# Split products whose moving operand is read as two halves in turns

## The chip, the cores and the metric

The kernel runs on one core of one Trainium2 chip. The metric is the device time of one execution in microseconds (us), of which the median of several runs is given. Beside it stands a profile of one execution with the start and the duration of every instruction on the core's engines: PE (TensorE, matrix products), PEld (the loading of TensorE's stationary operand, the weights, which runs beside PE), DVE (VectorE), ACT (ScalarE), POOL (GpSimd) and SP (SyncE, which issues the transfers).

## The reference

One layer of a decoder trunk, for 256 tokens of width 2048, all in float32. Cut to what matters here:

```python
mod = silu(c) @ w_ada + b_ada                       # six vectors of 2048
sh1, sc1, g1, sh2, sc2, g2 = split(mod, 6)
h = layer_norm(x) * (1 + sc1) + sh1
proj = h @ w_in                                     # 2048 x 9760
y_nsa, y_ml = nsa_attention(...), mlstm(...)        # of the columns of proj
g_nsa, g_ml = split(sigmoid(merge_g), 2)            # merge_g: 4096 columns of proj
y = (g_nsa * (y_nsa @ w_br_nsa) + g_ml * (y_ml @ w_br_ml)) @ w_o
x = layer_norm(ALPHA * x + g1 * y)
h = layer_norm(x) * (1 + sc2) + sh2
a, g = split(h @ w_up, 2)                           # 2048 x 11264
a = causal_dwconv(a)                                # width 3 along the tokens
y = (silu(a) * g) @ w_down                          # 5632 x 2048
x = layer_norm(ALPHA * x + g2 * y)
```

## The kernel before

A product of a float32 activation and a float32 weight is made of three matmuls in the type fp32r, here called a *split product*. Each operand is split in a high part (a cast to fp32r, on ACT) and a low part (the value less its high part, on DVE); the three matmuls are high by high, high by low and low by high, summed in PSUM. Weights come in tiles of 128 partitions by 1024 elements (512 KB, tile `w`), are split by `load_split` into `wh` (line L143, ACT) and `wl` (L146, DVE), and are used at once. Activations are split once and stay: `hT` (the input of all projections of `w_in`), `y_nsaT`, `y_mlT`, `mgT`, `h2T`, `uTt`, each laid out with the contracted dimension in the partitions and the 256 tokens along the free dimension, high half and low half apart.

All matmuls are issued by the helper `mm` (L109). In a matmul the stationary operand (128 columns) is loaded first, and then the moving operand streams past it, one column after the other; a column of the moving operand becomes a column of the result. There are two kinds of split products:

- `mm_b`: the weights are stationary and the 256 tokens of an activation are moving. The result has channels in the partitions and tokens in columns. It makes `ps_b` (the columns of `w_in` that attention needs transposed) and `ps_up` (the up projection).
- `mm_a`: 128 tokens are stationary and the weights are moving, 512, 392 or 256 columns of them. The result has tokens in the partitions. It makes `ps_a` (the rest of `w_in`), `ps_mg` (merge gates), `ps_br` (the two branch projections), `ps_o` (the output projection) and `ps_d` (the down projection). `proj_rows` does the last two; its last 512 columns go in two chunks of 256 (`_pack_rows` lays the weights out for it).

The order of time is: modulation, layer norm and `w_in` in three groups of its contracted dimension (to some 285 us); attention and mLSTM with `ps_mg` filled in between (to 440); `ps_br`, the rest of `ps_mg`, and `ps_o` (to 640); two layer norms (to 715); then `ps_up` for 22 blocks of 128 channels, `ps_d` over them, `ps_up` for 22 more and `ps_d` over those. Beside it `ada_chunk` multiplies the 100 MB of `w_ada` on DVE (L239, L257), a tile at a time, up to 935 us. The order of PE's work is in part written out by hand (`tc.manual_schedule`) and elsewhere follows the program; a scheduler with a cost model places the instructions of ACT and DVE.

Results leave PSUM in `dest_b` and the lines that use it (`ps_b`, L813, L815 and L817), in `residual_steps` (`ps_o`, `ps_d`), and in `up` (`ps_up`). In `up` a block of 128 channels goes through a bias and scale (L1546), the convolution along the tokens as two multiply-adds (L1549, one reads a shift of one token, the other of two), SiLU (L1551), the gate (L1552), and a split into `uTt` (L1554, L1555). The constants `OFFB`, `OFFA` and `OFFN` move the start of the tiles `wh`, `wl` and others by 16, 48 or 64 elements.

## Time and profile before

| | |
|---|---|
| median of 3 runs | 1427.51 us (1427.41 to 1427.63) |
| span of the profiled execution (first to last instruction) | 1425.4 us |
| PE busy | 1411.8 us (99%), 9234 matmuls |
| PEld busy | 1267.9 us (89%) |
| DVE busy | 1054.2 us (74%) |
| ACT busy | 704.2 us (49%) |
| moved by DMA | 374.23 MB, 263 GB/s on the mean |

The profiled execution's span ends 2.1 us under the median of the runs; the runs were not profiled, and hold what lies before the first and after the last instruction. In rows of the profile, `PE ps_up L109 x912` are 912 matmuls that write the PSUM tile `ps_up`, issued on line 109. The mean duration of a matmul counts its way through the array and is longer than its share of the time, since matmuls overlap; the distance from start to start, or a stretch divided by its count, says what one costs. A plain float32 product (not split) shows as two records for each matmul.

### The profile page before, as it was taken

What the parts mean: (1) busy time and instruction counts of PE and PEld (TensorE: products, weight loads), DVE (VectorE), ACT (ScalarE), POOL (GpSimd) and SP (SyncE); (2) the same over time, 40 slices, a digit from 0 to 9 for tenths busy, and PEclk for the clock granted to TensorE, in tenths of its full rate; (3) what the DMA queues carried; (4) which work ended last, traced back from release to release, by engine and by line L of the source; (5) the groups of instructions that cost most, each with busy time, mean ns of one, the idle gap of its engine ahead of it and who ended that gap; (6) DMA issues with size and microseconds to landing.
All of it is one profiled execution on the core that took longest, in us unless ns stands there. A gap on an engine that the chain in (4) does not pass through costs nothing.

```text
span 1425.4 us, 23418 instructions
## 1 busy us (share of the span) xinstructions
PE 1411.8 (99%) x9234; PEld 1267.9 (89%) x9234; DVE 1054.2 (74%) x1471; ACT 704.2 (49%) x969; POOL 3.6 (0%) x11
## 2 busy tenths in 40 slices
PE   7999999999999999999999999999999999999998
PEld 6999998877777888888799999988889999998887
DVE  8899977878787897789888777755555556555577
ACT  7644454645476434435755544443344444444341
POOL 0000000000000000000000000000000000000000
PEclk9999999999999999999999999999999999999999
DMA  9999978887877999996488878866666666666661
GB/s 379 418 419 365 374 256 286 317 283 237 291 267 278 340 328 339 342 329 224 139 323 288 279 249 293 271 192 193 191 192 194 194 195 193 195 196 193 194 195 72
DMA packets 103309, 374.23 MB, mean 263 GB/s; under 512 B 11168, under 2 KB 11680, under 8 KB 102432
## 3 DMA queue, kind: packets, MB, share of 16 engines
q1 hardware_dynamic: 103200, 372.75, 75.6%
q8 instruction: 72, 1.18, 0.3%
q14 instruction: 37, 0.30, 0.1%
HBM read 370.61 MB, written 2.10 MB: 261 GB/s over the span
## 4 chain that ended last, share of the span: by engine, by line
PE 93%; DVE 4%; DMA 1%; ACT 1%; issue 1%; SPq 0%; DVEq 0%; ACTq 0%
PE ps_up L109 32%; PE ps_d L109 17%; PE ps_mg L109 12%; PE ps_b L109 8%; PE ps_a L109 8%; PE ps_br L109 6%; PE ps_o L109 3%; PE ps_u L109 2%; PE ps_s L109 1%; PE ps_y L109 1%; DMA w<-in_w_o_dram 1%; DVE wl L146 1%; PE ps_hid L109 1%; PE ps_pT L989 0%; DVE w L257 0%
## 5 line engine op out<-in xcount | busy, mean ns | idle before, releaser
L146 DVE TENSOR_TENSOR wl<-w,wh 128x1024 fp32r<-128x1024 f32 (+1 forms) x470 | 564.9, 1206 | 325.2 <-ACT wh L143 324.2
L143 ACT CAST wh<-w 128x1024 fp32r<-128x1024 f32 (+1 forms) x470 | 486.4, 1038 | 598.0 <-PE ps_up L109 183.3
L109 PE MATMUL ps_up<-h2T,wh 128*128 128x256 f32 x2688 | 457.9, 276 | 0.0
L109 PEld LDWEIGHTS ps_up<-h2T,wh 128*128 128x128 f32 x2688 | 404.8, 188 | 0.2
L109 PE MATMUL ps_up<-h2T,wl 128*128 128x256 f32 x1344 | 371.2, 276 | 0.0
L109 PEld LDWEIGHTS ps_up<-h2T,wl 128*128 128x128 f32 x1344 | 252.3, 188 | 0.0
L109 PE MATMUL ps_d<-wh,uTt 128*128 128x512 f32 (+1 forms) x704 | 205.7, 376 | 0.0
L109 PE MATMUL ps_mg<-wh,hT 128*128 128x512 f32 x512 | 169.4, 401 | 0.0
L257 DVE SCALAR_TENSOR_TENSOR w<-w,crow 128x1024 f32<-128x1024 f32 x132 | 160.6, 1218 | 0.0
L109 PEld LDWEIGHTS ps_d<-wh,uTt 128*128 128x128 f32 x704 | 129.2, 188 | 23.9
L109 PE MATMUL ps_d<-wl,uTt 128*128 128x512 f32 (+1 forms) x352 | 132.1, 376 | 0.0
L109 PE MATMUL ps_b<-hT,wh 128*128 128x256 f32 x768 | 128.3, 280 | 3.1 <-ACT hT L417 2.8
L109 PEld LDWEIGHTS ps_b<-hT,wh 128*128 128x128 f32 x768 | 111.6, 189 | 7.0 <-ACT hT L417 3.5
L109 PEld LDWEIGHTS ps_mg<-wh,hT 128*128 128x128 f32 x512 | 96.2, 188 | 22.7 <-issue 3.1
L109 PE MATMUL ps_a<-wh,hT 128*128 128x392 f32 (+1 forms) x384 | 107.9, 359 | 0.0
L109 PE MATMUL ps_mg<-wl,hT 128*128 128x512 f32 x256 | 100.0, 391 | 0.0
L109 PE MATMUL ps_b<-hT,wl 128*128 128x256 f32 x384 | 92.4, 279 | 0.0
L109 PEld LDWEIGHTS ps_a<-wh,hT 128*128 128x128 f32 x384 | 70.7, 188 | 7.0 <-issue 1.8
L109 PEld LDWEIGHTS ps_d<-wl,uTt 128*128 128x128 f32 x352 | 66.1, 188 | 12.0
L109 PE MATMUL ps_a<-wl,hT 128*128 128x392 f32 (+1 forms) x192 | 68.8, 359 | 0.0
L109 PEld LDWEIGHTS ps_b<-hT,wl 128*128 128x128 f32 x384 | 67.3, 191 | 0.1
L109 PE MATMUL ps_o<-wh,mgT 128*128 128x512 f32 x192 | 59.5, 390 | 0.0
(316 smaller groups left out, 1325.5 us busy)
## 6 DMA issues: line engine op xcount, KB each, us to landing
w<-in_w_up_dram SPq DMA_DIRECT2D x176, 512.0 KB, 4.2
w<-in_w_ada_dram SPq DMA_DIRECT2D x132, 512.0 KB, 4.9
w<-in_w_down_dram SPq DMA_DIRECT2D x89, 512.0 KB, 3.6
w<-in_w_mg_dram SPq DMA_DIRECT2D x64, 512.0 KB, 4.8
w<-in_w_in_b_dram SPq DMA_DIRECT2D x48, 512.0 KB, 10.5
w<-in_w_br_dram SPq DMA_DIRECT2D x32, 512.0 KB, 5.2
w<-in_w_o_dram SPq DMA_DIRECT2D x32, 512.0 KB, 4.9
adaA<-in_w_ada_dram SPq DMA_DIRECT2D x15, 1024.0 KB, 11.1
```

Source lines behind the costliest of these rows:

```text
L109: nc.tensor.matmul(o, lhsT, rhs, start=start, stop=stop)
L143: hi = nc.scalar.copy(wh[:, :n], t[:, :n])
L146: lows.append(nc.vector.tensor_sub(wl[:, :n], t[:, :n], wh[:, :n]))
L257: ins = nc.vector.scalar_tensor_tensor(t, t, 1.0, crow[:, i * 1024:(i + 1) * 1024], op0=ALU.mult, op1=ALU.mult, accum_out=parts[:, row(m), ...
```

## The change

Each moving operand of a split product is read through `turns`: of its columns the first of the first half, the first of the second half, the second of the first half, and so on. So two neighbours in the stream lie half an operand apart (128 elements of 256, 256 of 512, 196 of 392), and column 2b+a of the result belongs to column b of half a.

In `mm_a` the weights are moving. They are laid out for it before the launch (`_even_odd` puts the even columns into the first half and the odd ones into the second), so the result's columns stand in their usual order. The vector `grow` that scales the last chunk of `w_down` is read in the same order (step 2).

In `mm_b` the tokens are moving, and the result's columns are tokens 0, 128, 1, 129 and so on. The lines that take `ps_b` out of PSUM read it with a step of 2 elements. In `up` the block stays in that order until the split: a shift of one token is a shift of two columns, and the first tokens of the second half take theirs from the last of the first half, which are two more multiply-adds of 1 and 2 columns for each block; the split reads with a step of 2. The two blocks that come by transposes (`j < 2`) are written to PSUM with a step of 2.

Not changed are the products `ps_u` (the first two blocks of the up projection), all plain float32 products, and the stationary operands.

```diff
+    def turns(ap):
+        return ap.rearrange("p (a b) -> p b a", a=2)
...
     def mm_b(ps, wh, wl, i, xt, k, start, stop):
         a, b = wh[:, i * P:(i + 1) * P], wl[:, i * P:(i + 1) * P]
-        mm(ps, a, xt[:, k, 0, :], start, False)
-        mm(ps, a, xt[:, k, 1, :], False, False)
-        mm(ps, b, xt[:, k, 0, :], False, stop)
+        xh, xl = [turns(xt[:, k, x, :]) for x in range(2)]
+        mm(ps, a, xh, start, False)
+        mm(ps, a, xl, False, False)
+        mm(ps, b, xh, False, stop)
 
     def mm_a(ps, xt, k, t, wh, wl, start, stop):
         xh, xl = xt[:, k, 0, t * P:(t + 1) * P], xt[:, k, 1, t * P:(t + 1) * P]
+        wh, wl = turns(wh), turns(wl)
...
-                src = (ps.rearrange("p (w t k) -> p w t k", w=2, t=2) if kind
-                       else ps.rearrange("p (a b) -> p a b", a=2))
+                dst, src = dest_b(b // 2), ps.rearrange("p (a k t) -> p a t k", a=2, t=2)
...
-                        nc.vector.tensor_mul(v, v, grow[:, c0:c0 + 256].rearrange(
-                            "p (o n) -> p o n", o=1).to_broadcast([P, m, 256]))
+                        vv = v.rearrange("p k (a b) -> p k a b", a=2)
+                        nc.vector.tensor_mul(vv, vv, grow[:, c0:c0 + 256].rearrange(
+                            "p (o b a) -> p o a b", o=1, a=2).to_broadcast([P, m, 2, P]))
...
-                    nc.tensor.transpose(ps[:, b * S + t * P:b * S + (t + 1) * P], ub[t][:, c:c + P], ident)
+                    nc.tensor.transpose(ps[:, b * S:(b + 1) * S].rearrange("p (k t) -> p t k", t=2)[:, t],
+                                        ub[t][:, c:c + P], ident)
...
+        aa, vv = [x.rearrange("p (k t) -> p t k", t=2) for x in (a, av)]
         for i in (1, 0):
             sh = 2 - i
-            nc.vector.scalar_tensor_tensor(av[:, sh:], a[:, :S - sh], fw(i), av[:, sh:],
+            nc.vector.scalar_tensor_tensor(av[:, 2 * sh:], a[:, :S - 2 * sh], fw(i), av[:, 2 * sh:],
+                                           op0=ALU.mult, op1=ALU.add)
+            nc.vector.scalar_tensor_tensor(vv[:, 1, :sh], aa[:, 0, P - sh:], fw(i), vv[:, 1, :sh],
                                            op0=ALU.mult, op1=ALU.add)
...
-        nc.scalar.copy(u[:, 0, :], av)
-        nc.vector.tensor_sub(u[:, 1, :], av, u[:, 0, :])
+        hi, lo = [uTt[:, j % KH, x, :].rearrange("p (t k) -> p t k", t=2) for x in range(2)]
+        nc.scalar.copy(hi, vv)
+        nc.vector.tensor_sub(lo, vv, hi)
...
+def _even_odd(w, cw):
+    K, N = w.shape
+    return w.reshape(K, N // cw, cw // 2, 2).swapaxes(2, 3).reshape(K, N)
...
-    r = [_pack_a(w[:, :1536], 512)]
+    r = [_pack_a(_even_odd(w[:, :1536], 512), 512)]
...
-    t[:K] = w[:, 1536:]
+    t[:K] = _even_odd(w[:, 1536:], 256)
```

PE, SP and POOL keep their instructions and the order of them, from the first to the last. Rows move on ACT and DVE alone, from the first block of `up` on. The first place is DVE in a block of the first 22, where `w,parts<-w,crow` is a step of `ada_chunk` and `wl` the low part of a weight tile. Before:

```order
L146 TENSOR_TENSOR wl<-w,wh 128x1024
L1549 SCALAR_TENSOR_TENSOR av<-ps_up,ffn,av 128x255
L1549 SCALAR_TENSOR_TENSOR av<-ps_up,ffn,av 128x254
L146 TENSOR_TENSOR wl<-w,wh 128x1024
L257 SCALAR_TENSOR_TENSOR w,parts<-w,crow 128x1024
L1552 TENSOR_TENSOR av<-av,ps_up 128x256
L146 TENSOR_TENSOR wl<-w,wh 128x1024
L1555 TENSOR_TENSOR uTt<-av,uTt 128x256
```

Behind each of the two multiply-adds there is now one of 1 or 2 columns, and nothing else is in another place. DVE in the same block of the changed kernel:

```order
L150 TENSOR_TENSOR wl<-w,wh 128x1024
L1558 SCALAR_TENSOR_TENSOR av<-ps_up,ffn,av 128x254
L1560 SCALAR_TENSOR_TENSOR av<-ps_up,ffn,av 128x1
L1558 SCALAR_TENSOR_TENSOR av<-ps_up,ffn,av 128x252
L1560 SCALAR_TENSOR_TENSOR av<-ps_up,ffn,av 128x2
L150 TENSOR_TENSOR wl<-w,wh 128x1024
L263 SCALAR_TENSOR_TENSOR w,parts<-w,crow 128x1024
L1563 TENSOR_TENSOR av<-av,ps_up 128x256
L150 TENSOR_TENSOR wl<-w,wh 128x1024
L1566 TENSOR_TENSOR uTt<-av,uTt 128x256
```

The second place is ACT at the same stage, where `wh` is the high part of a weight tile. Before:

```order
L143 CAST wh<-w 128x1024 x2
L1546 ACTIVATE av<-ps_up,ffn 128x256
L143 CAST wh<-w 128x1024
L1551 ACTIVATE av<-av 128x256
L143 CAST wh<-w 128x1024
L1554 CAST uTt<-av 128x256
```

The rows of a block are the same in the changed kernel, shown next; only for the first three blocks, which are done together, does a cast of `uTt` stand one weight tile later.

```order
L147 CAST wh<-w 128x1024 x2
L1554 ACTIVATE av<-ps_up,ffn 128x256
L147 CAST wh<-w 128x1024
L1562 ACTIVATE av<-av 128x256
L147 CAST wh<-w 128x1024
L1565 CAST uTt<-av 128x256
```

## The prediction

> **What bounds the kernel now.** I read the page's head first, then the chain that ended last, then the chain piece by piece, and last the busy time by stage.

> ```profile
> span 1425.4 us, 23418 instructions
> core 0: 1425.4 us, clock 0.998
> PE 93%; DVE 4%; DMA 1%; ACT 1%; issue 1%; SPq 0%; DVEq 0%; ACTq 0%
> PE ps_up L109 32%; PE ps_d L109 17%; PE ps_mg L109 12%; PE ps_b L109 8%; PE ps_a L109 8%; PE ps_br L109 6%; PE ps_o L109 3%; PE ps_u L109 2%; PE ps_s L109 1%; PE ps_y L109 1%; DMA w<-in_w_o_dram 1%; DVE wl L146 1%; PE ps_hid L109 1%; PE ps_pT L989 0%; DVE w L257 0%
> ```

> 93% of the chain is PE, and the changed tiles (`ps_up`, `ps_d`, `ps_mg`, `ps_b`, `ps_a`, `ps_br`, `ps_o`) are 86%. TensorE's granted clock is 0.998 of full, so there is nothing to win there. What a column of a moving operand costs decides the time. The chain, in order of time, gives it as a stretch and its count:

> ```profile
> 90.79 2.29 DVE adaA L239 x2
> 93.42 1.14 DVE wl L146
> 94.56 2.22 DVE adaB L239 x2
> ...
> 98.09 2.62 PE ps_b L109 x20
> 100.74 19.80 PE ps_b L109 x172
> 120.54 39.80 PE ps_a L109 x206
> 162.88 38.09 PE ps_b L109 x334
> 353.61 0.86 PE ps_y L109 x2
> 495.14 21.80 PE ps_br L109 x96
> 562.28 16.35 PE ps_mg L109 x72
> 605.15 32.44 PE ps_o L109 x143
> 829.82 0.87 PE ps_adar L293 x8
> 935.14 119.71 PE ps_d L109 x528
> 1054.85 239.58 PE ps_up L109 x2112
> 1294.43 120.89 PE ps_d L109 x660
> ```

> A split matmul of 512 columns takes 119.71 / 528 = 226.7 ns in `ps_d` (227.1 in `ps_br` and `ps_mg`, 226.9 in `ps_o`), one of 256 columns 239.58 / 2112 = 113.4 ns in `ps_up`. Half the columns, half the time: 0.443 ns for each column, and next to nothing for each matmul. Now `ps_y`: a plain float32 product of 512 columns, which shows as two records, takes 0.86 / 2 = 430 ns for each record, 0.840 ns a column. If a split column ran at just twice that pace it would take 0.420 ns, and 512 columns 215 ns. It takes 5.4% more. So either the factor is not two, or a split column pays something that a plain one, at its slower pace, hides.

> What that may be, a DVE row suggests. `xe` (L592) reads `accC` in steps of 16 elements, so that no two neighbours of its stream lie together:

> ```profile
> L592 DVE TENSOR_TENSOR xe<-accC,prm x8: 576/578/583, 197.7 to 226.2; 128x240 f32<-128x240 f32 x8
> L146 DVE TENSOR_TENSOR wl<-w,wh 128x1024 fp32r<-128x1024 f32 x438 | 534.5, 1223 | 316.1 <-ACT wh L143 315.2
> L1555 DVE TENSOR_TENSOR uTt<-av,uTt 128x256 fp32r<-128x256 f32 x44 | 18.3, 419 | 0.1
> ```

> Contiguous, 1024 elements take 1223 ns and 256 take 419: 1.047 ns an element and 151 fixed. The 240 scattered ones take (578 - 151) / 240 = 1.78 ns each. And four contiguous columns of a split product take 4 x 0.443 = 1.77 ns. The two figures agree within 1%. My reading, an inference from these rows: a read port opens one unit of four neighbouring elements at a time and needs 1.77 ns for it; DVE and the plain products, which use four elements in over 3.3 ns, don't notice, and the split products, which would use four in 1.68, wait for the memory. The change lets two units be used side by side, for eight columns (3.36 ns). Whether the openings of the two overlap is the question, and no row before shows such a stream on PE.

> **The change part by part.**

> *Moving operands.* If the two openings overlap, the memory no longer sets the pace, and a column costs what `ps_y` allows: 512 columns 215 ns, to which I add 1 for the wait between matmuls that a paced stream may show, 216. For 256 columns the weights come into play: each matmul loads its own 128 columns.

> ```profile
> 252.45 0.53 PEld L109 LDWEIGHTS ps_kc<-gT,w2t 128*128 128x128 f32 x4
> 252.90 0.19 PEld L109 LDWEIGHTS ps_a<-wl,hT 128*128 128x128 f32 x1
> ```

> `ps_kc` moves only 32 columns, so loading sets its pace: four loads from 252.45 to 252.90, 112 ns each. The transposes (`ps_adar`, 128 columns) go at 0.87 / 8 = 109 ns with a load each. So 256 columns can't come far below 109 to 112; I take 110, between the two and nearer to the lower, in which the loads run beside a full stream.

> Counts are those of the loops. `ps_up`: 42 blocks x 2 x 16 x 3 = 4032 matmuls, 113.4 to 110: 3.4 x 4032 = 13.7 us. 512 wide: `ps_d` 924, `ps_mg` 768, `ps_br` 384, `ps_o` 288, together 2364, 226.8 to 216: 25.5 us. `ps_b`: (19.80 + 38.09) / 506 = 114.4 ns, some 694 of them from 98 us on: 3.1 us. `ps_a` from 120 us on: 156 of 512 columns at 10.8 ns (1.7) and 312 of 392 columns at 0.0211 x 392 = 8.3 ns (2.6), 4.3 us. The 256 wide ones of `ps_d` (264) and `ps_o` (192) at 3.4: 1.6 us. Sum 48.2 us. What runs before 98 us is left out: there PE ends up waiting for DVE's products of `w_ada` (the `adaA` and `adaB` pieces), whatever its own pace.

> What of it is lost, by stage (columns: length, then busy us of PE, PEld, DVE, ACT, POOL, clock, DMA share, GB/s):

> ```profile
> 100.00:160.00 60.00, 59.98 (x385) 57.26 (x384) 56.73 (x69) 26.65 (x32) 0.00 (x0) 1.00 0.99 386
> 430.00:600.00 170.00, 170.00 (x767) 140.08 (x766) 137.54 (x181) 78.87 (x90) 0.00 (x0) 1.00 0.89 322
> 716.00:830.00 114.00, 114.00 (x1009) 114.00 (x1008) 88.39 (x124) 58.95 (x80) 0.00 (x0) 1.00 0.82 284
> 830.00:935.00 105.00, 105.00 (x928) 105.00 (x927) 78.94 (x110) 52.22 (x69) 0.00 (x0) 1.00 0.81 272
> 1055.00:1295.00 240.00, 240.00 (x2115) 239.87 (x2114) 142.02 (x176) 115.72 (x152) 0.00 (x0) 1.00 0.64 194
> ```

> From 100 to 160 us DVE works 56.73 of 60 and the DMA engines 0.99 of the time: a faster PE would wait for them. I take back that stage's share, 172 x 4.4 ns + 206 x 9.1 ns = 2.6 us, and 0.7 us for the 192 narrow `ps_o` matmuls, beside which DVE works on the residual. Elsewhere DVE is at 59 to 84% and the DMA at most at 0.89 (322 of the 386 GB/s seen above), so 5% less time for the same work still fits. Net 45 us.

> *Two more multiply-adds for each block of `up`* (88 in all), 1 or 2 columns each. The nearest row is a multiply-add of one column:

> ```profile
> L194 DVE SCALAR_TENSOR_TENSOR rs_n<-rs_n 128x1 f32<-128x1 f32 x2 | 0.4, 220 | 0.1
> L1549 DVE SCALAR_TENSOR_TENSOR av<-ps_up,ffn,av 128x254 f32<-128x254 f32 x44 | 21.0, 481 | 1.5
> ```

> 88 x 0.22 = 19.4 us of DVE, half of it in the first 22 blocks (9.7), where DVE is idle for 219 - 167.33 = 51.7 us; the first weight tiles behind a block get their low part 0.44 us later, under tiles that are some 2.7 us of PE apart (24 matmuls at 113.4). Cost nothing; were there no idle time, 19.4 us.

> *Reads with a step of 2* (the split into `uTt`, the copies and sums out of `ps_b`, the scaling by `grow`). No row has this step. Lower end: nothing, since a step of 2 still uses two elements of each unit of four. Upper end: each element its own opening, 1.78 ns, by which L1555 goes from 419 to 607 ns, 8.3 us in 44, and a `ps_b` sum of 512 columns to 151 + 911 = 1062 ns. I take nothing, as the step is nearer to contiguous than to 16; at the upper end the `ps_b` sums from 100 to 160 us would cost that stage, which has DVE idle for 3.3, up to 2 us.

> *The eight transposes into PSUM with a step of 2*: no row writes so. 109 ns each, 0.9 us in all; I take no change, and 1 us at the upper end.

> Sum: 1425.4 - 45 = 1380.4 us for a profiled execution, and 2.1 more, the distance of the median from the span before: 1382.5.

> By itself the likeliest case reaches from 1367 (narrow ones at 107.5, wide ones at 215: 5.9 x 4032 + 11.8 x 2364 and the rest in step, 60 us) to 1398 (112 and 219: 5.6 + 18.4 + 5, 29 us).

> **The rivals.**

> *Nothing is kept between turns (slower).* If the port holds one unit only, each column of the alternating stream opens one anew, and costs 1.78 ns as in L592 in place of 0.443. The changed matmuls move 2.9 million columns (4032 x 256 + 2364 x 512 and the rest); 1.34 ns more for each is 3.9 ms, and the kernel would take some 5300 us. It decides as soon as a column in turns costs more than 0.443 ns. For it speaks that L592 is the only scattered stream in the trace and pays in full; against it, that L592 never comes back to a unit, while here each is wanted again two columns later.

> [...]

> *Nothing changes.* Two units for eight columns are as many openings as one for four. If the port opens them one after the other, 0.443 ns stays, and so does the time, 1427.5. The same comes out if the 5.4% is not the memory's at all.

> *A part only.* Loads hold the 256 wide ones at 112 or above, and half of the excess stays on the wide ones (221 ns): 2364 x 5.7 + 4032 x 1.4 and some 3 elsewhere are 22 us: 1405.

> *A dearer start (slower).* The last piece of `ps_d` above holds 396 wide matmuls (89.8 us at 226.7) and 264 narrow ones, which so take 31.1 / 264 = 117.8 ns, 4.4 more than in `ps_up`. So where an operand begins matters, and streams in turns begin in two places. 4.4 ns on all 8580 changed matmuls is 38 us: 1465.

> **How the numbers follow.** The agreement of 1.78 with 1.77 ns makes the memory's share of the 5.4% likely, and a stream that returns to both units makes overlap likelier than loss: gain in full 0.52, a part 0.12, nothing 0.12, dearer start 0.09, nothing kept 0.15. A measurement of this kernel tells 0.2% (2.9 us) from no change: faster 0.64, same 0.12, slower 0.24. The predicted time is that of the first case, 1383. The range reaches from its lower end, 1367, over the part and no change to the dearer start, 1468, and leaves out the last rival.

> **What would show it.** Right: `ps_d` pieces of the chain at 215 to 219 ns a matmul, `ps_up` at 109 to 112, and the same chain otherwise, with new DVE or DMA pieces at most from 100 to 160 us. Wrong: `ps_d` at 227 (no overlap), wide ones quicker but `ps_up` at 113 (the loads are the bound there, 14 us less gain), anything above 240 (units lost), or L1549 and L1555 in the chain.

## The result and the profile after

The changed kernel takes 1386.01 us (median of 4 runs, 1385.72 to 1386.57) against 1427.46 for the kernel before (4 runs, 1427.38 to 1427.63): a ratio of 0.9709, 95% interval 0.9695 to 0.9722, so 2.9% faster. The forecast was 1383 with a range of 1367 to 1468.

The head of the page after, its summary of the chain that ended last, and the chain's long pieces in order of time (start us, length us, engine, tile, line, count):

```profile
span 1384.2 us, 23506 instructions
PE 1364.6 (99%) x9234; PEld 1252.2 (90%) x9234; DVE 1059.6 (77%) x1559; ACT 705.6 (51%) x969; POOL 3.6 (0%) x11
PE 84%; DVE 7%; DMA 5%; issue 2%; ACT 1%; SPq 0%; DVEq 0%; ACTq 0%
```

```profile
100.68 15.69 PE ps_b L109 x138
160.87 37.29 PE ps_b L109 x334
480.06 20.72 PE ps_br L109 x96
543.97 15.54 PE ps_mg L109 x72
584.79 30.88 PE ps_o L109 x143
908.97 113.96 PE ps_d L109 x528
1022.93 235.84 PE ps_up L109 x2112
1258.77 75.13 PE ps_d L109 x348
```

The number of matmuls is the same, and each of the changed ones costs less. Those of 512 columns went from 226.7 to 113.96 / 528 = 215.8 ns in `ps_d`, and to 215.8, 215.8 and 215.9 in `ps_br`, `ps_mg` and `ps_o`. Those of 256 went from 113.4 to 235.84 / 2112 = 111.7 ns in `ps_up`, and in `ps_b` from 114.0 to 111.6 (the piece of 334). Half the columns are now more than half the time (111.7 against 215.8 / 2 = 107.9 ns), where the straight order had 113.4 against 113.35: a cost for each matmul now shows.

Where the 41.2 us of the span went, by the starts of the same pieces before and after:

| stage | before, us | after, us | gained |
|---|---|---|---|
| up to the second group's `ps_b` | 0 to 100.74 | 0 to 100.68 | 0.1 |
| second group (`ps_b`, `ps_a`) | to 162.88 | to 160.87 | 2.0 |
| third group | to 284.92 | to 278.45 | 4.5 |
| attention, mLSTM, `ps_mg` | to 442.31 | to 429.75 | 6.1 |
| `ps_br`, `ps_mg`, first `ps_o` | to 605.15 | to 584.79 | 7.8 |
| rest of `ps_o`, layer norms, `ps_u` | to 715.30 | to 692.61 | 2.3 |
| first `ps_up` | to 935.14 | to 908.97 | 3.5 |
| first `ps_d` | to 1054.85 | to 1022.93 | 5.8 |
| second `ps_up` | to 1294.43 | to 1258.77 | 3.7 |
| second `ps_d` and the end | to 1425.4 | to 1384.2 | 5.5 |

The gain lies in every stage in which PE sets the pace, and the stages with 512 columns have most of it. What is late next shows in two places. From 100 to 160 us DVE and the DMA engines are nearly full (columns: length, then busy us of PE, PEld, DVE, ACT, POOL, clock, DMA share, GB/s):

```profile
100.00:160.00 60.00, 59.33 (x392) 56.66 (x392) 57.17 (x70) 27.46 (x32) 0.00 (x0) 1.00 1.00 391
```

And at the end the chain has left PE, which the prediction had not expected there. After the 348 matmuls of `ps_d` it goes through a weight tile's transfer and then over DVE's scaling and splitting of the last tiles (four pieces of it, in order of time):

```profile
1336.25 4.35 DMA w<-in_w_down_dram
...
1342.16 1.20 DVE wl L150
...
1344.50 1.32 DVE w L1251
...
1359.42 0.67 DVE w L1251
```

The second `ps_d` still gained what its matmuls' paces give (396 x 10.9 ns + 264 x 5.4 = 5.7 us, against 5.5), so next to nothing is lost there yet.

### The profile page after: what moved, and what is told of

It reads as the page before. It is cut to its first block, busy times and chain, and to the rows that moved or that the text cites. A ratio compares the mean times of both kernels' runs of the same rounds, so it can differ in the third digit from the quotient of the medians.

```text
span 1384.2 us, 23506 instructions
## 1 busy us (share of the span) xinstructions
PE 1364.6 (99%) x9234; PEld 1252.2 (90%) x9234; DVE 1059.6 (77%) x1559; ACT 705.6 (51%) x969; POOL 3.6 (0%) x11
## 4 chain that ended last, share of the span: by engine, by line
PE 84%; DVE 7%; DMA 5%; issue 2%; ACT 1%; SPq 0%; DVEq 0%; ACTq 0%
PE ps_up L109 33%; PE ps_d L109 14%; PE ps_mg L109 12%; PE ps_br L109 6%; PE ps_a L109 6%; PE ps_b L109 5%; PE ps_o L109 3%; DVE wl L150 2%; DMA w<-in_w_in_b_dram 2%; PE ps_u L109 2%; DMA w<-in_w_in_a_dram 1%; PE ps_s L109 1%; PE ps_y L109 1%; DMA adaA<-in_w_ada_dram 1%; DMA w<-in_w_o_dram 1%
## 5 line engine op out<-in xcount | busy, mean ns | idle before, releaser
L109 PE MATMUL ps_up<-h2T,wh 128*128 128x256 f32 x2688 | 450.7, 275 | 0.0
L109 PEld LDWEIGHTS ps_up<-h2T,wh 128*128 128x128 f32 x2688 | 408.7, 192 | 0.1
L109 PE MATMUL ps_up<-h2T,wl 128*128 128x256 f32 x1344 | 369.7, 275 | 0.0
L109 PEld LDWEIGHTS ps_up<-h2T,wl 128*128 128x128 f32 x1344 | 258.0, 192 | 0.0
L109 PE MATMUL ps_d<-wh,uTt 128*128 128x512 f32 (+1 forms) x704 | 198.5, 366 | 0.0
L109 PE MATMUL ps_mg<-wh,hT 128*128 128x512 f32 x512 | 163.1, 389 | 0.0
L109 PEld LDWEIGHTS ps_d<-wh,uTt 128*128 128x128 f32 x704 | 129.9, 189 | 16.4
L109 PE MATMUL ps_d<-wl,uTt 128*128 128x512 f32 (+1 forms) x352 | 128.8, 366 | 0.0
L109 PE MATMUL ps_b<-hT,wh 128*128 128x256 f32 x768 | 124.9, 277 | 3.8 <-ACT hT L423 2.8
L109 PEld LDWEIGHTS ps_b<-hT,wh 128*128 128x128 f32 x768 | 110.9, 192 | 7.7 <-ACT hT L423 3.5
L109 PEld LDWEIGHTS ps_mg<-wh,hT 128*128 128x128 f32 x512 | 96.8, 189 | 16.0 <-issue 3.1
L109 PE MATMUL ps_a<-wh,hT 128*128 128x392 f32 (+1 forms) x384 | 103.6, 348 | 0.6 <-ACT wh L147 0.6
L109 PE MATMUL ps_mg<-wl,hT 128*128 128x512 f32 x256 | 97.2, 380 | 0.0
L109 PE MATMUL ps_b<-hT,wl 128*128 128x256 f32 x384 | 90.7, 275 | 0.0
L109 PEld LDWEIGHTS ps_a<-wh,hT 128*128 128x128 f32 x384 | 69.4, 189 | 6.2 <-issue 2.2
L109 PEld LDWEIGHTS ps_d<-wl,uTt 128*128 128x128 f32 x352 | 66.7, 189 | 8.4
L109 PE MATMUL ps_a<-wl,hT 128*128 128x392 f32 (+1 forms) x192 | 67.0, 350 | 1.3 <-DVE wl L150 1.2
L109 PEld LDWEIGHTS ps_b<-hT,wl 128*128 128x128 f32 x384 | 67.5, 192 | 0.1
L109 PE MATMUL ps_o<-wh,mgT 128*128 128x512 f32 x192 | 57.3, 379 | 0.0
```

The source lines that it names most:

```text
L109: nc.tensor.matmul(o, lhsT, rhs, start=start, stop=stop)
```

## The experiments

The prediction's mechanism (called theory U from here on: a port opens a unit of four neighbouring elements in 1.77 ns, and two open units used side by side hide that) was the open question; that the time came out close does not show it. Ten variants of the changed kernel were run. All but the last two have a single time; the kernel before stood at 1427.47 beside the first four and at 1427.8 or 1427.4 beside the others.

**Four columns a turn.**

```diff
-        return ap.rearrange("p (a b) -> p b a", a=2)
+        return ap.rearrange("p (a b c) -> p b a c", a=2, c=4)
```

> The changed kernel, but each turn takes four neighbouring columns of a half before the other half has its turn. (The result's columns stand in other places than in the reference, here and in the next three.) Theory U: a read port opens units of four neighbouring elements in 1.77 ns each, and the gain comes from using two open units side by side. Then this order, which uses up a unit before it wants the next, gains nothing: 512 columns at 226 to 228 ns, 256 at 113 to 114, span about 1425 us. Rival B: neighbouring units lie in one part of the memory that can't be opened twice in quick succession, and units half an operand apart can. Then this order gains all: 216 and 111.7 ns, span about 1384 us.

**Turns within eight neighbours.**

```diff
-        return ap.rearrange("p (a b) -> p b a", a=2)
+        return ap.rearrange("p (g a b) -> p g b a", a=2, b=4)
```

> The changed kernel, but the turns are taken within every eight neighbouring columns: columns 0, 4, 1, 5, 2, 6, 3, 7, then 8, 12 and so on. Theory U (two units side by side): 512 columns at 216 ns, 256 at 111.7, span about 1384 us, since the distance doesn't matter. Rival B (neighbouring units hinder each other): 226 to 228 and 113 to 114 ns, span about 1425 us.

**Quarters and eighths.** The same line with `a=4`, and with `a=8`.

> The changed kernel, but four quarters of the operand take turns, one column each. Theory U with two units kept: each column opens its unit anew, 1.78 ns, 512 columns at some 910 ns and a time near 5200 us. Theory U with four units kept or more: 216 and 111.7 ns, span about 1384 us. Rival B: as with two halves, 1384 us.

> The changed kernel, but eight eighths of the operand take turns, one column each. Theory U with fewer than eight units kept: each column opens its unit anew, 512 columns at some 910 ns and a time near 5200 us. With eight kept: 216 and 111.7 ns, span about 1384 us. Rival B: 1384 us.

The first `ps_d` piece of the chain of each, in the order four a turn, next units, quarters, eighths:

```profile
1016.58 132.01 PE ps_d L109 x528
```

```profile
908.86 113.96 PE ps_d L109 x528
```

```profile
1124.56 149.58 PE ps_d L109 x528
```

```profile
1764.08 256.97 PE ps_d L109 x528
```

That is 250.0, 215.8, 283.3 and 486.7 ns a matmul, and 1560.39, 1385.56, 1735.21 and 2748.85 us. The next units gain all, so the distance of half an operand is not needed, and rival B, that neighbouring units hinder each other, falls. Theory U does not come through either: four columns a turn should have cost what the straight order costs, 227 ns, and took 250; and the quarters and eighths are neither at 216 nor at 910.

**Pairs in turns.** Theory U has two open units here, used side by side as in the change; under E each path leaves its unit after every column.

```diff
-        return ap.rearrange("p (a b) -> p b a", a=2)
+        return ap.rearrange("p (a b c) -> p b a c", a=2, c=2)
```

> The changed kernel, but each turn takes two neighbouring columns of a half (result columns in other places, as in the next one). Theory E, formed after the four runs before: the stream is read by two paths, one for its columns 0, 2, 4, the other for 1, 3, 5, each with one open unit of its own; what counts is how many columns in a row a path takes from one unit: four in the changed kernel and in the turns of next units (no cost), two in the straight order (6%) and in turns of four (18%), one in the quarters (33%). With pairs in turns each path leaves its unit after every column: as the quarters, 512 columns at 270 to 300 ns, 256 at 135 to 150, span 1650 to 1800 us. Theory U (two open units for the whole stream, used side by side): 216 and 111.7 ns, span about 1384 us.

```profile
1312.12 175.99 PE ps_d L109 x528
1488.11 358.75 PE ps_up L109 x2112
```

333.3 and 169.9 ns, 2032.16 us. Theory U (216) is dead. E has the direction, and its size was too small (270 to 300 expected).

**Turns within a unit**, 0, 2, 1, 3: two in a row for each path, as in the straight order.

```diff
-        return ap.rearrange("p (a b) -> p b a", a=2)
+        return ap.rearrange("p (g a b) -> p g b a", a=2, b=2)
```

> The changed kernel, but the turns are taken within every four neighbouring columns: 0, 2, 1, 3, then 4, 6, 5, 7. Theory E: each path takes two columns from a unit, as in the straight order: 226 to 228 and 113 to 114 ns, span about 1425 us. Rival C: the cost of the straight order comes from columns that follow their direct neighbour; here two of four steps are no such neighbours, so at most half of it stays: 221 ns, span 1405 us or less.

```profile
935.25 119.71 PE ps_d L109 x528
1054.96 239.58 PE ps_up L109 x2112
```

226.7 and 113.4 ns, 1427.44 us: the straight order's figures to the digit, though the order is another. As E says, and rival C (221) falls.

**Two in a row, far apart.** Here neighbours of the stream lie in different units, as in the change (512 elements apart, there 256), but each path takes only two columns of a unit.

```diff
+        if ap.shape[-1] == 1024:
+            return ap.rearrange("p (a n c) -> p n c a", a=2, c=4)[:, :, 0:2, :]
         return ap.rearrange("p (a b) -> p b a", a=2)
...
-                        mm_a(pss[t], xT, k, t, wh[:, j * 512:(j + 1) * 512],
-                             wl[:, j * 512:(j + 1) * 512], k == 0, k == kn - 1)
+                        mm_a(pss[t], xT, k, t, wh, wl, k == 0, k == kn - 1)
```

> The changed kernel, but the 512 wide matmuls of ps_mg, ps_br, ps_o and ps_d read, in turns, two halves of a whole weight tile of 1024 elements, and of each four neighbours only the first two (half the weights are left out, the others used twice). Neighbours in the stream so lie 512 elements apart, and each of the two paths of theory E takes two columns from a unit and goes on to the next unit. Theory E (what counts is how many columns in a row a path takes from a unit; a unit takes 1.77 ns to open, and two columns of one path are used up in 1.67): 226 to 228 ns, as in the straight order, span about 1410 us. Rival G (what counts is that two columns that are read together come from different units): 215 to 217 ns, span about 1384 us.

```profile
925.10 119.73 PE ps_d L109 x528
1044.83 235.84 PE ps_up L109 x2112
```

226.8 ns again for the wide ones, 1411.94 us, while the narrow ones, left in turns, keep 111.7. That neighbours in the stream come from different units is thus not enough; four columns in a row for each path, as E has it, fits.

**Shorter loads of the weights.** Why do 256 columns take 111.7 ns when 512 take 215.8?

```diff
+    cut = []
+
     def mm_b(ps, wh, wl, i, xt, k, start, stop):
...
-        mm(ps, a, xh, start, False)
-        mm(ps, a, xl, False, False)
-        mm(ps, b, xh, False, stop)
+        n = P // 2 if cut and not (start or stop) else P
+        mm(ps[:n], a[:, :n], xh, start, False)
+        mm(ps[:n], a[:, :n], xl, False, False)
+        mm(ps[:n], b[:, :n], xh, False, stop)
...
+    cut.append(1)
```

(`cut` is filled ahead of the up projection.)

> The changed kernel, but of the 48 matmuls of each half block of the up projection only the first and the last have 128 stationary columns, the others 64 (half the channels are left out of the sums). Theory L: the 256 wide matmuls stand at 111.7 ns because the next 128 weight columns take that long to load, and the moving operand would allow 215.9 / 2 = 108. Then the up projection goes at 108 ns, 4032 x 3.7 = 15 us less, span about 1369 us. Rival: 111.7 ns is what 256 columns and a fixed cost for each matmul take; then the span stays at 1384 us.

The chain piece and the load group:

```profile
1019.74 231.22 PE ps_up L109 x2112
```

```profile
L109 PEld LDWEIGHTS ps_up<-h2T,wh 128*64 128x64 f32 x2352 | 288.5, 136 | 0.0
```

The time is 1378.33 us, between the two forecasts. Behind a matmul of 64 stationary columns the next one starts 109 or 110 ns later, 109.2 on the mean of 3444; the piece's mean of 231.22 / 2112 = 109.5 has the full ones in it. So a matmul of 128 stationary columns takes 111.7 in place of 109.2, but under that lies no 108: two widths, 215.83 for 512 (the changed kernel, granted clock 1.000) and 109.17 for 256 (this run, 0.998), give as an estimate (215.83 - 109.17) / 256 = 0.417 ns a column and 2.5 ns for each matmul.

Theory L is not borne out as it was put. Where a matmul of 64 columns is followed by one of 128, whose load runs beside it, the step is still 109 or 110 ns (84 cases); where one of 128 is followed by one of 64, it is 111 or 112 (83 of 84 cases). So the difference of 109.2 and 111.7 goes with the width of the matmul that is running, and not with the load beside it. The run also halves the partitions that such a matmul writes; what makes the difference is open.

**Turns only where weights are moving.**

```diff
-        xh, xl = [turns(xt[:, k, x, :]) for x in range(2)]
+        xh, xl = [xt[:, k, x, :] for x in range(2)]
...
-                    mm(o, wh, turns(hT[:, k0 + k, 0, :]), opening, False)
-                    mm(o, wl, turns(hT[:, k0 + k, 0, :]), False, False)
+                    mm(o, wh, hT[:, k0 + k, 0, :], opening, False)
+                    mm(o, wl, hT[:, k0 + k, 0, :], False, False)
```

> The changed kernel with the 256 wide matmuls of the up projection and of ps_b, whose moving operand is the activation, read in straight order again; turns only where weights are moving (result columns of those two in other places). By the sum as measured (113.5 against 111.7 ns for 4032 up products, 7.2 us, and some 3 us for ps_b): about 1396 us, ratio to the kernel before 0.978. By the sum as it was predicted (3.4 ns for each, 13.7 and 3.1 us): about 1403 us, ratio 0.983.

1395.51 us (4 runs, 1395.25 to 1397.71), ratio 0.9777 (0.976 to 0.9793): the first of the two forecasts. The moving weights bring some 32 us of the 41, the moving activations 9.5.

**Without the small multiply-adds.**

```diff
-            nc.vector.scalar_tensor_tensor(vv[:, 1, :sh], aa[:, 0, P - sh:], fw(i), vv[:, 1, :sh],
-                                           op0=ALU.mult, op1=ALU.add)
```

> The changed kernel without the two added multiply-adds of 1 and 2 columns in each block of the up projection (so the first two tokens of the second half lack part of their convolution). As predicted they cost nothing, being beside DVE's idle time: 1385 to 1387 us, ratio to the kernel before as the changed kernel's, 0.971. Rival: they delay the low parts of the weights behind them, 88 times 0.21 us at most: down to 1368 us, ratio 0.958.

1387.11 us (1385.6 to 1390.43), ratio 0.9725 (0.9709 to 0.9741), against 0.9709 (0.9695 to 0.9722) with them. They cost nothing that can be measured.

## Why the prediction was right

**The pace of the wide matmuls** carried the sum, and came out as put: 216 forecast, 215.8 measured, 10.9 x 2364 = 25.8 us against 25.5. It rested on `ps_y` (half a plain pass of 430 ns) and on 1 ns for a wait between matmuls, which was the author's estimate and stood in no row.

**The pace of the narrow ones** is the step that was mis-sized. 110 ns was taken between 109 and 112; it is 111.7, the upper end, which `ps_kc` had shown for 128 columns of weights loaded back to back. The nearer row was `ps_kc` (112) and not the transposes (109), though both load 128 columns for each matmul, and the run with shorter loads does not bear out that the loading beside the stream is the reason. `ps_up` brought 1.77 x 4032 = 7.1 us in place of 13.7, and `ps_b`, from 114.4 to some 111.6, 1.9 in place of 3.1.

**Two smaller terms** came out higher. The 392 wide `ps_a` went from a median of 178 ns, start to start, to 166, 12 in place of 8.3 for each. And the narrow `ps_d` went from 117.8 to 112.4, since what the last rival feared as a dearer start vanished instead: in the straight order most narrow matmuls stand at 113 or 114 ns and those of some tiles at 117 to 120, and in turns nearly all stand at 111 or 112.

**What was taken back for the stage from 100 to 160 us**, 2.6 us, was too much: it gained 2.0, with DVE at 57.17 of 60. With the two smaller terms this makes up for about half of what the narrow matmuls lack: 41.2 us of the profiled span measured, 45 forecast. That the time came within 3 us of the forecast is owed in part to errors that went against each other.

**What was to be hidden was hidden.** The two new groups on DVE (line, operation, shape, count, busy us, mean ns, idle before):

```profile
L1560 DVE SCALAR_TENSOR_TENSOR av<-ps_up,ffn,av 128x2 f32<-128x2 f32 x44 | 9.2, 210 | 0.0
L1560 DVE SCALAR_TENSOR_TENSOR av<-ps_up,ffn,av 128x1 f32<-128x1 f32 x44 | 9.2, 208 | 0.0
```

18.4 us of DVE against 19.4 put, and none of it in the time. One sign that was named for being right did not come: new DVE and DMA pieces were to stand in the chain at most from 100 to 160 us, and they stand before 100 us and from 1333.92 us to the end as well.

**The reason given was right in part only.** That the straight order's 5% belongs to how the operand is read is shown: the order of reading alone moves the pace from 215.8 to 487 ns. The price of 1.77 ns for a unit fits the straight order (from which it was taken, 4 x 0.443), turns within a unit (226.7 ns) and two in a row far apart (226.8): by theory E a path, to which every second column goes, uses two columns of a unit in 2 x 2 x 0.417 = 1.67 ns and waits for 1.77. It fits the change and the next units, both at 215.8, where a path would take four, have 3.34 ns and wait for nothing. It does not fit four columns a turn, also two in a row for each path, at 250. Whether DVE's 1.78 in L592 is more than a coincidence no run tests.

What the prediction had wrong is one port with two units in use. Two paths with a walk of their own are an inference, but the pairs speak for them: the same two units side by side as in the change, eight columns from them, and 333 ns. So it was luck that the change takes one column of each half in turns: "two units side by side" would have allowed the pairs too, and with them 2032 us. The case against the first rival held for two streams only: eight cost 487 ns, above the straight order's 227 and in the direction of that rival.

Open is what a path does with one column in a row. With one unit kept and 1.77 ns for each opening, 512 columns would take 256 x 1.77 = 453 ns by that estimate; quarters take 283, pairs 333, eighths 487. The first two suggest that more than one unit is kept or opened ahead, and the last that an opening can cost more than 1.77; how many are kept was not tried. Nor is it settled why two in a row cost 250 with a jump of half an operand between units and 227 when the next unit follows.

## What to carry to other kernels

Compare the pace of a column in matmuls of the same engine at different rates (here split products at 0.443 ns a column against plain ones at 0.840): a cost that grew with the columns and not with the matmuls pointed to how the operand is read. That is cheap to test, since the order of a moving operand can be changed by its access pattern and a new layout of the weights, and a wrong order is dear (up to 2749 us here). What helped split products here was an order in which the even columns of the stream came from one stretch of memory and the odd ones from another, at least four in a row from each; turns within eight neighbours did as well as halves (1385.56 us and 1386.01). Before counting a gain for narrow matmuls, look for the next bound in a row with the same stationary operand: here 112 ns in `ps_kc`, less than 2 ns below the old pace.

## What the runs showed that was not expected

Reads with a step of 2 were put at nothing. Out of PSUM that held (the sums of `ps_b`, L823, take 688 and 683 ns, before 688 and 677). Out of SBUF it did not on ACT: the cast into `uTt` (before and after)

```profile
L1554 ACT CAST uTt<-av 128x256 fp32r<-128x256 f32 x44 | 17.5, 403 | 1.3
```

```profile
L1565 ACT CAST uTt<-av 128x256 fp32r<-128x256 f32 x44 | 21.4, 489 | 2.0 <-DVE av L1563 0.3
```

pays 86 ns for 256 elements. On DVE the subtraction of the same operand went from 419 to 430 ns, and the scaling by `grow`, with a stepped and repeated operand, from 1221 to 1369 ns on the mean (the first of the five took 1536, the others 1321 to 1343; after):

```profile
L1251 DVE TENSOR_TENSOR w<-w,g 128x1024 f32<-128x1024 f32 x5 | 6.8, 1369 | 1.9 <-DMA w<-in_w_down_dram 1.9
```

These 0.8 us lie on DVE's work at the end of the kernel, which the chain now runs through.
